# The last pass of a gMLP and cross-attention layer: only TensorE's order written by hand, rows of x three blocks deep, blocks of z two deep, and its entry, weight loads and raw tiles laid out anew

## The chip, the core and the metric

One core of a Trainium2 chip runs the whole kernel. The metric is the device time of one execution in microseconds (us), the median of several runs. The engines are named as in the profile: PE is TensorE's matmul, PEld its weight load, DVE is VectorE, ACT ScalarE, POOL GpSimd, and SP the engine whose queue issues every DMA of this kernel, in order.

## The reference, cut to what matters

One layer (DEPTH = 1) over x of 4096 rows and 1024 columns, all in float32:

```python
proj = einsum('bsd,de->bse', x, a_w_in)              # 1024 -> 768 + 768 + 256 + 1024
u, v, q_x, gate = split_cols(proj, [768, 768, 256, 1024])
tok = chunked_spatial_gating(u, v, a_w_s, a_b_s)     # gelu, norm by head, 128x128 causal mix, times u
xo = memory_cross_attention(q_x, mem_k, mem_v)       # 4 heads of 64 over a memory of 256 rows
mixed = concatenate([tok, xo]) * silu(gate)
y = einsum('bse,ed->bsd', mixed, w_out)              # 1024 -> 1024
x = layer_norm(ALPHA * x + y, ln_g, ln_b)            # over the 1024 columns of each row
```

## The kernel before

Rows are taken in 16 blocks of 256. A float32 operand is split into two parts that TensorE can multiply (`split`, L69: ACT copies the high part into the tile, then DVE subtracts it from the source and writes the low part), and a product of two split operands is three matmuls for each of four slices of the depth. The large products are done by a scheme of the Strassen kind with seven products in place of eight: sums and differences of the quarters of a block (`x_parts`, on POOL, into three `sums` tiles) are split into seven tiles of a ring (`ringp`, seven buffers named `xc`), and each of the seven is multiplied by one of seven weight tiles of 128 x 4096 elements, which lie in one large tile (`arena`). Such a product is 12 matmuls.

There are four passes over the blocks. Passes 0 and 1 (loop over `g`, L289) compute u, v, q and a part of the gate, and write them to DRAM. Beside them they prepare the weights of later passes (`prepare_slice`), split them and store them to DRAM (`wd`, `wgd`), and pass 1 computes the keys and values of the memory (`memory`, L244) with tiles of its own (`mr`, `wr`, `wt`). The third pass, here the attention pass (L393 to L538), computes the rest of the gate and the attention and writes z, the product of mixer and gate, to DRAM (`z_d`). It reads back three of the four quarters of x as split tiles (`load_x`: `xc` from `xd`), and the fourth, `a21`, raw (`x21` from `xT`), which it splits itself; after `a21` the ACT queue holds the softmax. The last pass (L541 to L727) multiplies z by `w_out`, adds x and normalizes.

Blocks of x and z come through `raw` tiles (L60, three buffers of half a block), of which a block takes two. What the planner does not decide is set by `manual_schedule`: inside it the named engines keep the order of the code. In the attention pass that is PE alone; in the last pass it was PE, DVE, ACT and POOL. Everything else, and above all SP's queue, stands in the order in which the planner put it at build time. An engine and a queue work strictly in order: what waits at the head holds all behind it.

In the last pass, block b goes through products P0 to P6, in the order of the code: `accw`, `accx`, `accq`, `accw`, `accx`, `accq`, `accw` (three accumulators; `accw` is taken up again by P3 and P6, `accx` by P4, `accq` by P5). Between them DVE reads the accumulators: t12 after P0 (`plus`, L634, from the block's rows of x, `xr`), t22 after P2, x22 after P3, x11 after P4, x12 after P5, x21 after P6; ACT copies `accx` to s1 after P1; POOL adds s1 to t12, t22 and x21. P3 can't start before t12 has read its accumulator, P5 not before t22, P6 not before x22. Beside that, the parts of block b+1 are summed on POOL and split (`nxt.sums`, `nxt.part`), and block b-1, two tiles n0 and n1 of 128 rows, is normalized: `mean` and `var` on ACT with sums along the row, a power on POOL, `norm` on ACT (one pass of 128 x 1024), `gain` and `shift` on DVE (128 x 1024 each), and then the DMA of the rows to `out`. The rows of x lie in `xr`, four tiles, that is two blocks; the tile of block b+1 is the one out of which block b-1 has just been written.

Of the kernel before, what the change touches and what calls it, by code (L numbers as in the profile page):

```python
# [35 lines left out]
def trunk_kernel(ctx, tc, xT, x, memT, w_kv, wl, wsT, bsT, ln_g, ln_b, out):  # L36
# [23 lines left out]
    def raw_tile():  # L60
        return stagep.tile([P, KH, 2 * P], F32, name="raw", tag="raw", bufs=3)
# [4 lines left out]
    def cs_tile():  # L66
        return stagep.tile([P, 512], F32, name="cs", tag="cs", bufs=6)
# [56 lines left out]
    def view(off, n):  # L124
# [8 lines left out]
        3: [13312, 17408, 21504, 25600, 0, 4096, 8192],  # L133
# [46 lines left out]
    def weights(g, load=()):  # L180
        ws = [view(o, WIDTH[g]) for o in places[g]]
        for i in load:
            nc.sync.dma_start(f(ws[i]), w_d[g][i])
        return ws
# [59 lines left out]
    def memory(pool, psum):  # L244
# [6 lines left out]
        for k in range(KD):  # L251
            mr = pool.tile([P, M], F32, name="mr")
            nc.sync.dma_start(mr, memT[:, k, :])
            wr = pool.tile([P, 2 * M], F32, name="wr")
# [3 lines left out]
            wt = pool.tile([P, 2, 2 * M], F32R, name="wt")  # L258
# [30 lines left out]
    for g in range(2):  # L289
        with tc.tile_pool(name=f"mix{g}", bufs=1, reuse_waits="tile") as pool, \  # L290
# [21 lines left out]
            for b in range(NB):  # L312
# [14 lines left out]
                if g == 1 and b == 3:  # L327
                    memory(pool, psum)
# [62 lines left out]


    with tc.tile_pool(name="att", bufs=1, reuse_waits="tile") as pool, \  # L393
# [8 lines left out]
        def x21_tile():  # L402
            return pool.tile([P, KH, P], F32, name="x21", bufs=2)

        x21s = [x21_tile()]
# [8 lines left out]
        def load_x(b):  # L414
# [4 lines left out]
            raw = x21s.pop() if x21s else x21_tile()  # L419
# [73 lines left out]
        gx = None  # L493
        with tc.manual_schedule(engines={mybir.EngineType.PE}):
            for b in range(NB):
                xs = nxt
                z1s = [load_z(b, j) for j in range(2)]
# [22 lines left out]
                gate(0, 0, 0)  # L520
                gate(0, 0, 1)
# [3 lines left out]
                gate(1, 0, 0)  # L525
                turn(p0, 0, 0)
                gate(1, 0, 1)
                turn(p1, 1, 0)
                gate(0, 1, 0)
                gate(0, 1, 1)  # L530
                turn(p2, 0, 1)
                gate(1, 1, 0)
                turn(p3, 1, 1)
                gate(1, 1, 1)
# [6 lines left out]
    with tc.tile_pool(name="fin", bufs=1, reuse_waits="tile") as pool, \  # L541
            tc.tile_pool(name="acc3", bufs=8, space=bass.MemoryType.PSUM, reuse_waits="tile") as psum:
        ws = weights(3, range(3, 7))
        H = D // 2
        xr, blocks = {}, {}

        def rows(b, i):

            for a in range(4):
                yield slice(a * 32, (a + 1) * 32), b * TB + (a % 2) * P + (2 * i + a // 2) * 32  # L550

        def load_xr(b):
            for i in range(2):
# [215 lines left out]
```

## Time and profile before

| what | value |
|---|---|
| runs | 1573.48, 1571.53, 1570.72 us; median 1571.53 |
| the profiled execution | 1573.17 us, of which the profile's span is 1571.40 |
| PE, DVE, ACT, POOL busy, share of the span | 89%, 66%, 47%, 42% |
| passes 0 and 1 | start to about 752 us |
| attention pass | about 765 to 1141 us |
| last pass | 1141 us to the end |

The row on the granted clock in the profile's second part stands at 9 (tenths of full speed) nearly throughout, with single slices at 7 where the passes meet. The digits of PE are 9 from slice 2 on and fall to 8 in the last pass. Times in the trace are microseconds from the span's start.

### The profile page before, as it was taken

How to read it: one execution, taken by the hardware profiler on the slowest of the kernel's cores; microseconds unless marked ns; L12 is line 12 of the kernel's file. 1: busy time of each engine (PE TensorE's matmuls, PEld its weight loads, DVE VectorE, ACT ScalarE, POOL GpSimd, SP SyncE). 2: the span in 40 equal slices, each digit the busy share in tenths (PEclk: the TensorE clock that was granted, in tenths of full speed). 3: DMA queues.
4: the chain of work that ended last, by engine and by line, in shares of the span. 5: the costliest groups of instructions: out<-in, count | busy, mean ns of one | idle time of the engine just before them, and what ended most of it. 6: DMA issues, size and time to landing. Idle time of an engine off the chain costs nothing.

```text
span 1571.4 us, 20805 instructions
## 1 busy us (share of the span) xinstructions
PE 1399.9 (89%) x6720; PEld 1178.0 (75%) x6720; DVE 1034.1 (66%) x2098; ACT 746.2 (47%) x1597; POOL 658.4 (42%) x515
## 2 busy tenths in 40 slices
PE   2799999999999999999499999999969888888884
PEld 2677776777778878878399999999947666666663
DVE  5788778777478867776256666666635656565555
ACT  4555555555355555555154444444515444444442
POOL 4645443444254345443044333433524454544442
PEclk9899999999999999999799999999979999999997
DMA  6468677756988585858977777777683444353523
GB/s 200 139 175 218 168 224 202 197 144 201 359 265 279 185 281 184 274 168 260 401 240 210 205 201 204 191 209 191 168 288 94 124 118 136 106 150 104 148 77 98
DMA packets 313326, 305.88 MB, mean 195 GB/s; under 512 B 147072, under 2 KB 275328, under 8 KB 310912
## 3 DMA queue, kind: packets, MB, share of 16 engines
q1 hardware_dynamic: 313216, 304.55, 66.0%
q8 instruction: 53, 0.87, 0.2%
q14 instruction: 57, 0.47, 0.1%
HBM read 183.38 MB, written 121.11 MB: 194 GB/s over the span
## 4 chain that ended last, share of the span: by engine, by line
PE 37%; DVE 18%; DMA 17%; POOL 8%; issue 7%; ACT 6%; SPq 5%; POOLq 0%; ACTq 0%; DVEq 0%
PE gate L189 16%; PE accw L189 7%; DVE xc L71 5%; PE accx L189 5%; PE accq L189 3%; DMA xr<-x 3%; DMA out<-xr 2%; DMA raw<-xT 2%; ACT vg L379 2%; DMA raw<-wl 2%; PE at L471 2%; PE sc L433 2%; ACT xc L70 2%; PE pt L451 2%; POOL cs L689 2%
## 5 line engine op out<-in xcount | busy, mean ns | idle before, releaser
L189 PE MATMUL accw<-arena,xc 128*128 128x512 f32 x1728 | 455.1, 413 | 93.5 <-ACT xc L70 34.1
L189 PEld LDWEIGHTS accw<-arena,xc 128*128 128x128 f32 x1728 | 334.3, 197 | 187.5 <-ACT xc L70 36.6
L189 PE MATMUL accx<-arena,xc 128*128 128x512 f32 x1152 | 299.8, 402 | 17.5 <-ACT arena L70 12.1
L189 PE MATMUL gate<-arena,xc 128*128 128x384 f32 x1536 | 291.4, 342 | 13.6 <-ACT xc L70 13.6
L189 PE MATMUL accq<-arena,xc 128*128 128x512 f32 x1152 | 292.2, 398 | 10.1 <-DVE cs L634 10.0
L189 PEld LDWEIGHTS gate<-arena,xc 128*128 128x128 f32 x1536 | 265.7, 190 | 14.0 <-ACT xc L70 13.8
L189 PEld LDWEIGHTS accx<-arena,xc 128*128 128x128 f32 x1152 | 218.2, 192 | 72.8 <-ACT arena L70 12.5
L189 PEld LDWEIGHTS accq<-arena,xc 128*128 128x128 f32 x1152 | 215.1, 189 | 64.4 <-DVE cs L634 14.9
L71 DVE TENSOR_TENSOR xc<-sums,xc 128x512 fp32r<-128x512 f32 x192 | 155.0, 809 | 136.1 <-ACT xc L70 135.5
L70 ACT CAST xc<-sums 128x512 fp32r<-128x512 f32 x192 | 118.2, 617 | 215.2 <-POOL sums L576 92.8
L71 DVE TENSOR_TENSOR xc<-raw,xc 128x512 fp32r<-128x512 f32 x144 | 112.1, 779 | 27.8 <-ACT xc L70 27.8
L511 POOL TENSOR_TENSOR z<-z,cs 128x384 f32<-128x384 f32 x64 | 72.5, 1133 | 131.7 <-DVE cs L509 70.6
L379 ACT ACTIVATE vg<-vg,nm,rs 128x128 f32<-128x128 f32 x192 | 77.7, 483 | 73.9 <-DVE nm L376 73.8
L70 ACT CAST xc<-raw 128x512 fp32r<-128x512 f32 x144 | 88.8, 616 | 25.9 <-PE accw L189 13.3
L445 POOL TENSOR_TENSOR sums<-sums,sm 128x512 f32<-128x512 f32 x48 | 49.3, 1041 | 98.5 <-DVE sm L444 93.9
L79 POOL TENSOR_TENSOR sums<-raw 128x512 f32<-128x512 f32 x32 | 43.2, 1350 | 109.2 <-DMA raw<-xT 62.0
L375 POOL TENSOR_TENSOR rs<-rs,mhalf 128x6 f32<-128x6 f32 x32 | 48.4, 1512 | 94.2 <-DVE rs L374 94.1
L715 POOL TENSOR_TENSOR xr<-xr,cs 128x512 f32<-128x512 f32 x16 | 26.1, 1633 | 126.5 <-DVE xr L634 125.6
L442 ACT ACTIVATE sums<-sc,nm 128x256 f32<-128x256 f32 x96 | 44.3, 472 | 67.1 <-DVE nm L438 67.1
L615 ACT ACTIVATE xr<-xr,nmean,rs 128x1024 f32<-128x1024 f32 x32 | 39.8, 1243 | 65.0 <-DVE nmean L614 53.9
L689 POOL TENSOR_TENSOR cs<-cs 128x512 f32<-128x512 f32 x16 | 26.2, 1638 | 105.3 <-DVE cs L634 105.3
L84 POOL TENSOR_TENSOR sums<-raw 128x512 f32<-128x512 f32 x32 | 45.4, 1419 | 54.1 <-DVE xc L71 51.8
(128 smaller groups left out, 2011.4 us busy)
## 6 DMA issues: line engine op xcount, KB each, us to landing
raw<-xT SPq DMA_DIRECT2D x64, 512.0 KB, 5.8
wd<-wc SPq DMA_DIRECT2D x56, 512.0 KB, 4.8
arena<-wd SPq DMA_DIRECT2D x14, 2048.0 KB, 14.2
xd<-xc SPq DMA_DIRECT2D x48, 512.0 KB, 4.8
xc<-xd SPq DMA_DIRECT2D x48, 512.0 KB, 4.5
raw<-wl SPq DMA_DIRECT2D x38, 512.0 KB, 4.1
raw<-zd SPq DMA_DIRECT2D x32, 512.0 KB, 3.9
xr<-x SPq DMA_DIRECT2D x128, 128.0 KB, 3.1
```

The source lines that it names most:

```text
L70: nc.scalar.copy(hi, src)
L71: nc.vector.tensor_tensor(lo, src, f(hi), op=ALU.subtract)
L79: tt(s1, a21, a22, op=ALU.add)
L84: tt(s3, a11, a21, op=ALU.subtract)
L189: nc.tensor.matmul(acc, t[:, a, k, :], w[:, b, k, :], start=first and k == 0 and i == 0, stop=last and k == KH - 1 and i == 2, skip_group_ ...
L375: nc.gpsimd.tensor_tensor(rs, rs, mhalf.rearrange("p (h c) -> p h c", c=2), op=ALU.pow)
L379: nc.scalar.activation(vg[:, h, c, :], vg[:, h, c, :], AF.Identity, bias=nm[:, h, c:c + 1], scale=rs[:, h, c:c + 1])
L442: nc.scalar.activation(p[:, e, :], ps[:, e, :], AF.Exp, bias=nm[:, e:e + 1], scale=SCALE, accum_out=sm[:, e:e + 1])
L445: nc.gpsimd.tensor_tensor(p, p, sm.unsqueeze(2).broadcast_to([P, 2, M]), op=ALU.mult)
L511: nc.gpsimd.tensor_tensor(z, z, g, op=ALU.mult)
L615: nc.scalar.activation(self.r, self.r, AF.Identity, bias=self.nmean, scale=self.rs)
L689: add(t22, t22, s1, op=ALU.add)
```

## The change

- **Tiles and pools.** `raw` tiles: four buffers for three; `cs` tiles five for six. `memory` takes its staging from `raw` and `wc` tiles and has none of its own. The `wc` pool is closed after pass 1, and in its place stands a pool for two `xr` tiles (`first_xr`). The fourth quarter of x in the attention pass is a `raw` tile (the left half of its columns) for the `x21` tile.
- **Weights of the last pass.** Weights 0 to 2 are loaded in blocks 4, 7 and 10 of the attention pass, ahead of its gates, and pinned there in program order (before: called after blocks 3, 6 and 9, and free for the planner). In the last attention block the gates of the second half come first, and weights 3 and 4 are loaded in the middle of that block into the places that these set free. The places of weights 3 to 5 change for that.
- **Depth.** Rows of x: block 0 and every third block use `first_xr`, the others four tiles of the last pass, so that a tile is taken again after three blocks. Pairs of z are loaded two blocks ahead (`pairs`), the first two during the last two attention blocks.
- **Order.** Only PE's order is by hand in the last pass.
- **Normalization.** `norm` is gone: `gain` is (r + nmean) * lg and `shift` is r * rs + lb, both scalar_tensor_tensor on DVE over 128 x 1024. The calls of n0 and n1 stand elsewhere in the code.

```diff
@@ pools
-    wring = ctx.enter_context(tc.tile_pool(name="wring", bufs=2))
+    front = ExitStack()
+    wring = front.enter_context(tc.tile_pool(name="wring", bufs=2))
-        return stagep.tile([P, KH, 2 * P], F32, name="raw", tag="raw", bufs=3)
+        return stagep.tile([P, KH, 2 * P], F32, name="raw", tag="raw", bufs=4)
-        return stagep.tile([P, 512], F32, name="cs", tag="cs", bufs=6)
+        return stagep.tile([P, 512], F32, name="cs", tag="cs", bufs=5)
-        3: [13312, 17408, 21504, 25600, 0, 4096, 8192],
+        3: [13312, 17408, 21504, 0, 4096, 25600, 8192],
@@ memory
-            mr = pool.tile([P, M], F32, name="mr")
+            raw = raw_tile().rearrange("p k c -> p (k c)")
+            mr, wr = raw[:, :M], raw[:, M:3 * M]
@@ between pass 1 and the attention pass
+    front.close()
+    first_xr = ctx.enter_context(tc.tile_pool(name="xr0", bufs=2, reuse_waits="tile"))
+    def load_z_pair(b):
+        zv = z_d[b].rearrange("k p t -> p k t")
+        return load_pair(zv[:, :KH, :], zv[:, KH:, :])
@@ attention pass
-            raw = x21s.pop() if x21s else x21_tile()
+            raw = raw_tile()[:, :, :P]
+                order = ((0, 0), (1, 0), (0, 1), (1, 1))
+                if b == NB - 1:
+                    order = ((0, 1), (1, 1), (0, 0), (1, 0))
                 if b + 1 < NB:
                     nxt = load_x(b + 1)
+                if b in (4, 7, 10):
+                    weights(3, (b // 3 - 1,), pinned=True)
+                if b == NB - 3:
+                    load_xr(0, first_xr, 2)
+                elif b >= NB - 2:
+                    pairs.append(load_z_pair(b - NB + 2))
...
+                if b == NB - 1:
+                    weights(3, (3, 4))
...
-                if b in (3, 6, 9):
-                    weights(3, (b // 3 - 1,))
@@ last pass
-        ws = weights(3, range(3, 7))
+        ws = weights(3, (5, 6))
-            def norm(self):
-                nc.vector.tensor_tensor(self.nmean, self.nmean, self.rs, op=ALU.mult)
-                nc.scalar.activation(self.r, self.r, AF.Identity, bias=self.nmean, scale=self.rs)
             def gain(self):
-                nc.vector.tensor_tensor(self.r, self.r, lg, op=ALU.mult)
+                nc.vector.scalar_tensor_tensor(self.r, self.r, self.nmean, lg, op0=ALU.add, op1=ALU.mult)
             def shift(self):
-                nc.vector.tensor_tensor(self.r, self.r, lb, op=ALU.add)
+                nc.vector.scalar_tensor_tensor(self.r, self.r, self.rs, lb, op0=ALU.mult, op1=ALU.add)
-        with tc.manual_schedule(engines={T_.PE, T_.DVE, T_.Activation, T_.Pool}):
+        with tc.manual_schedule(engines={mybir.EngineType.PE}):
             for b in range(NB):
-                    load_xr(b + 1)
+                    if (b + 1) % 3:
+                        load_xr(b + 1, pool, 4)
+                    else:
+                        load_xr(b + 1, first_xr, 2)
+                if b + 2 < NB:
+                    pairs.append(load_z_pair(b + 2))
```

Where this moves instructions is seen in the built programs. First SP's queue where the attention pass begins. In these rows `wgd`, `kd`, `qd` are weights, keys and queries of that pass, `xd` the split quarters of x, `x_7243` the raw fourth quarter of block 0, `wd_0` to `wd_2` the weights 0 to 2 of the last pass (2 MB each). Before:

```order
L418 DMA xc<-xd_2_156 128x1024
L490 DMA arena<-kd_203 128x1024
L426 DMA arena<-qd_106 128x4x256
L183 DMA arena<-wd_0_79 128x4096
L183 DMA arena<-wd_1_80 128x4096
L183 DMA arena<-wd_2_81 128x4096
L390 DMA z1d_104<-u 256x1x384
L239 DMA gxd_137<-gt 32x8x64 x4
L390 DMA z1d_105<-u 256x1x384
L426 DMA arena<-qd_107 128x4x256
L420 DMA x_7243<-xT 128x4x128
```

Now, at the same place, `raw` from `xT` by L442 being the fourth quarter:

```order
L440 DMA xc<-xd_2_156 128x1024
L512 DMA arena<-kd_203 128x1024
L448 DMA arena<-qd_106 128x4x256
L442 DMA raw<-xT 128x4x128
L412 DMA xr<-x 32x1024 x3
L442 DMA raw<-xT 128x4x128
L412 DMA xr<-x 32x1024 x2
L440 DMA xc<-xd_0_157 128x1024
L412 DMA xr<-x 32x1024 x3
L440 DMA xc<-xd_1_158 128x1024
```

The three weight loads are gone from here: `wd_0` now stands between the raw quarter of block 5 and the split quarters of block 2, `wd_1` between those of blocks 8 and 5, `wd_2` between those of blocks 11 and 8, about three blocks earlier than they are called. The raw quarter of block 0 stands 26 rows above the load of `qd_106`, in pass 1, those of blocks 1 and 2 behind it; the two shown here are of blocks 3 and 4. And eight loads of block 0's `xr` (128 KB each) stand here.

Second, the same queue in the middle of the last pass, with the numbers of the tiles: `xr_11785` and `xr_11790` are the two tiles of block 3 in the program before, `zd6` and `zd7` the blocks 6 and 7 of z. Before:

```order
L110 DMA raw_12306<-zd6_144 128x4x256
L556 DMA xr_11965<-x 32x1024 x4
L111 DMA raw_12307<-zd6_144 128x4x256
L623 DMA out<-xr_11785 32x1024 x4
L556 DMA xr_12135<-x 32x1024 x4
L623 DMA out<-xr_11790 32x1024 x4
L110 DMA raw_12481<-zd7_145 128x4x256
```

Here `xr_12135` is a tile of block 5. Now, with `xr_11777` and `xr_11782` the tiles of block 3 and `xr_12290`, `xr_12295` those of block 6:

```order
L113 DMA raw_12130<-zd6_144 128x4x256
L639 DMA out<-xr_11777 32x1024 x4
L412 DMA xr_12290<-x 32x1024 x4
L112 DMA raw_12300<-zd7_145 128x4x256
L639 DMA out<-xr_11782 32x1024 x4
L412 DMA xr_12295<-x 32x1024 x4
L113 DMA raw_12301<-zd7_145 128x4x256
```

Behind the output of block 3 stood the rows of block 5, now those of block 6; beside it stood the second half of z of block 6, now that of block 7 is loaded.

Third, DVE in one block of the last pass as it now stands, from t12 of block 4 (`cs_11999`) to x12 of block 4; `xc` rows are the splits of block 5's parts 0 to 4, L634 and L637 are gain and shift of n1 of block 2 (`xr_11611`), by the planner's order:

```order
L658 SCALAR_TENSOR_TENSOR cs_11999<-xr_11777,accw_11962 128x512
L615 TENSOR_SCALAR nmean_11946<-nmean_11946 128x1
L73 TENSOR_TENSOR xc_12007<-sums_11983,xc_12007 128x512
L620 TENSOR_SCALAR rs_11947<-rs_11947 128x1
L634 SCALAR_TENSOR_TENSOR xr_11611<-xr_11611,nmean_11946,lg_11429 128x1024
L73 TENSOR_TENSOR xc_12030<-raw_11787,xc_12030 128x512
L637 SCALAR_TENSOR_TENSOR xr_11611<-xr_11611,rs_11947,lb_11430 128x1024
L658 SCALAR_TENSOR_TENSOR cs_12045<-xr_11782,accq_12010 128x512
L73 TENSOR_TENSOR xc_12053<-sums_11982,xc_12053 128x512
L722 TENSOR_TENSOR xr_11782<-accw_11962,cs_12045 128x512
L73 TENSOR_TENSOR xc_12073<-sums_12056,xc_12073 128x512
L658 SCALAR_TENSOR_TENSOR xr_11777<-xr_11777,accx_11986 128x512
```

The rows that belong to one stretch of the program before, from its t12 on (`cs_12357`); L614 is the small product that ACT's `norm` waited for:

```order
L634 SCALAR_TENSOR_TENSOR cs_12357<-xr_12135,accw_12320 128x512
L600 TENSOR_SCALAR rs_12303<-rs_12303 128x1
L71 TENSOR_TENSOR xc_12363<-sums_12341,xc_12363 128x512
L71 TENSOR_TENSOR xc_12381<-raw_12306,xc_12381 128x512
L614 TENSOR_TENSOR nmean_12302<-nmean_12302,rs_12303 128x1
L595 TENSOR_SCALAR nmean_12304<-nmean_12304 128x1
L634 SCALAR_TENSOR_TENSOR cs_12400<-xr_12140,accq_12366 128x512
L71 TENSOR_TENSOR xc_12404<-sums_12340,xc_12404 128x512
L618 TENSOR_TENSOR xr_11960<-xr_11960,lg_11425 128x1024
L600 TENSOR_SCALAR rs_12305<-rs_12305 128x1
L697 TENSOR_TENSOR xr_12140<-accw_12320,cs_12400 128x512
```

Before, n0 was multiplied by the gain only after t22; now n0 is finished before t12 and n1 between t12 and t22.

## Rows read from the trace of the kernel before

**Rows 1.** Busy time by stage: length, then engines busy, PE clock, DMA share, GB/s
```profile
752.00:806.00 54.00, 31.10 (x166) 29.42 (x165) 18.28 (x46) 16.17 (x40) 10.61 (x10) 0.75 0.90 337
806.00:1141.00 335.00, 334.20 (x2153) 331.57 (x2152) 217.85 (x469) 159.94 (x454) 135.02 (x125) 1.00 0.75 201
1164.60:1551.60 387.00, 336.00 (x1308) 257.98 (x1308) 224.24 (x347) 169.13 (x267) 173.77 (x135) 0.94 0.43 120
1551.60:1571.40 19.80, 0.04 (x1) 0.00 (x0) 11.87 (x20) 2.48 (x2) 2.36 (x3) 0.62 0.32 83
```

**Rows 2.** Timeline of the start: start, duration, engine, line, operation, [idle before <-releaser]
```profile
22.12 1.26 POOL L79 TENSOR_TENSOR sums<-raw 128x512 f32<-128x512 f32 x1 [2.95 <-DMA raw<-xT]
...
48.44 0.79 PE L189 MATMUL accx<-arena,xc 128*128 128x512 f32 x1 [12.08 <-ACT arena L70]
```

**Rows 3.** Timeline where the attention pass begins, block 0
```profile
753.15 3.44 SPq L183 DMA_DIRECT2D arena<-wd  x3
...
766.61 4.87 PE L189 MATMUL gate<-arena,xc 128*128 128x384 f32 x24
...
785.39 0.62 ACT L70 CAST xc<-x 128x512 fp32r<-128x512 f32 x1 [25.89 <-DMA x<-xT]
...
786.06 4.29 PE L189 MATMUL gate<-arena,xc 128*128 128x384 f32 x12 [13.62 <-ACT xc L70]
```

**Rows 4.** Timeline of the attention pass: block 1's first gate, and one `xc` load ahead of block 14
```profile
805.95 4.33 PE L189 MATMUL gate<-arena,xc 128*128 128x384 f32 x24
...
1066.03 2.87 SPq L418 DMA_DIRECT2D xc<-xd  x2
```

**Rows 5.** Where the last pass begins: two timeline rows, one row of 3 us windows
```profile
1163.87 0.69 DVE L634 SCALAR_TENSOR_TENSOR cs<-xr,accw 128x512 f32<-128x512 f32 x1 [18.96 <-DMA xr<-x]
...
1164.61 5.49 PE L189 MATMUL accw<-arena,xc 128*128 128x512 f32 x12 [14.91 <-DVE cs L634]
...
1148.00:1151.00 3.00, 1.70 (x8) 1.03 (x6) 0.00 (x0) 0.65 (x2) 0.00 (x0) 1.00 1.00 426
```

**Rows 6.** Last pass: PE's P3, P5 and the next P3; waits after 1160 us
```profile
1411.16 3.03 PE L189 MATMUL accw<-arena,xc 128*128 128x512 f32 x12 [2.43 <-ACT junk L599]
...
1419.24 3.07 PE L189 MATMUL accq<-arena,xc 128*128 128x512 f32 x12 [1.55 <-DVE cs L634]
...
1437.44 5.46 PE L189 MATMUL accw<-arena,xc 128*128 128x512 f32 x12 [3.23 <-DVE rs L600]
...
DVE cs L634 <- DMA xr<-x: 32.6, 15, 19.0
```

**Rows 7.** Groups from 1160 us on: line, operation, count, busy us, mean ns
```profile
L615 ACT ACTIVATE xr<-xr,nmean,rs 128x1024 f32<-128x1024 f32 x32 | 39.8, 1243 | 65.0 <-DVE nmean L614 53.9 <-DMA out<-xr 11.1
L621 DVE TENSOR_TENSOR xr<-xr,lb 128x1024 f32<-128x1024 f32 x32 | 39.4, 1231 | 0.1
...
L71 DVE TENSOR_TENSOR xc<-raw,xc 128x512 fp32r<-128x512 f32 x45 | 31.0, 690 | 22.3 <-ACT xc L70 22.3
...
L576 POOL TENSOR_TENSOR sums<-raw 128x512 f32<-128x512 f32 x15 | 19.3, 1289 | 0.0
```

**Rows 8.** Timeline: DVE and POOL at the same moment, both with two operands in SBUF
```profile
1394.25 2.31 DVE L618 TENSOR_TENSOR xr<-xr,lg 128x1024 f32<-128x1024 f32 x1
...
1395.44 2.25 POOL L690 TENSOR_TENSOR cs<-cs 128x512 f32<-128x512 f32 x1
```

**Rows 9.** Timeline of the end: last matmuls, DVE's last statistics and last instruction
```profile
1548.68 2.96 PE L189 MATMUL accw<-arena,xc 128*128 128x512 f32 x12
...
1560.64 1.28 DVE L607 BATCH_NORM_STATS2 st<-xr 128x6 f32<-128x512 f32 x2
...
1565.80 1.23 DVE L621 TENSOR_TENSOR xr<-xr,lb 128x1024 f32<-128x1024 f32 x1
```

**Rows 10.** DMA groups of the page: issues, KB each, median us to landing
```profile
xc<-xd SPq DMA_DIRECT2D x48, 512.0 KB, 4.5
...
raw<-zd SPq DMA_DIRECT2D x32, 512.0 KB, 3.9
```

More of the change, by code (lines that the diff above doesn't have):

```diff
@@ L493, in trunk_kernel @@
         gx = None
+        pairs = []
         with tc.manual_schedule(engines={mybir.EngineType.PE}):
@@ L542, in trunk_kernel @@
             tc.tile_pool(name="acc3", bufs=8, space=bass.MemoryType.PSUM, reuse_waits="tile") as psum:
-        ws = weights(3, range(3, 7))
+        ws = weights(3, (5, 6))
         H = D // 2
[L545 to L553, printed above, removed]
-                t = xr[b, i] = pool.tile([P, D], F32, name="xr", bufs=4)
-                for s, r0 in rows(b, i):
-                    nc.sync.dma_start(t[s, :], x[r0:r0 + 32, :])
+        blocks = {}
         class Parts:
             def __init__(self, b):
-                self.r0, self.r1 = load_pair(z_d[b].rearrange("k p t -> p k t")[:, :KH, :],
-                                             z_d[b].rearrange("k p t -> p k t")[:, KH:, :])
+                self.r0, self.r1 = pairs[b]
                 self.tiles = []
@@ L675, in trunk_kernel @@
                 n0.var()
+                n1.mean()
                 nxt.part(0)
@@ L681, in trunk_kernel @@
                 nc.scalar.copy(s1, ax)
+                n0.gain()
+                n1.var()
                 nxt.part(1)
-                n0.norm()
-                n1.mean()
                 product(aw, xs[3], ws[3], False)
@@ L689, in trunk_kernel @@
                 add(t22, t22, s1, op=ALU.add)
-                add(t12, t12, s1, op=ALU.add)
+                n0.shift()
                 nxt.part(2)
-                n0.gain()
-                n1.var()
                 nxt.sums(3)
@@ L697, in trunk_kernel @@
                 nc.vector.tensor_tensor(x22, aw, t22, op=ALU.add)
+                add(t12, t12, s1, op=ALU.add)
+                n1.gain()
                 nxt.part(3)
-                n0.shift()
-                n1.norm()
                 product(aq, xs[5], ws[5], False)
@@ L705, in trunk_kernel @@
                 nxt.part(4)
-                n1.gain()
+                n1.shift()
                 product(aw, xs[6], ws[6], False)
@@ L710, in trunk_kernel @@
                 nxt.part(5)
-                n1.shift()
-                def last(aw=aw, x21=x21, s1=s1):
-                    plus(x21, aw, x21)
-                    add(x21, x21, s1, op=ALU.add)
-                n0, n1 = Norm(b, 0), Norm(b, 1)
+                n0, n1, last = Norm(b, 0), Norm(b, 1), Last(aw, x21, s1)
                 cur = nxt
             n0.stats()
-            n0.norm()
-            last()
             n0.gain()
             n0.shift()
+            last.c21()
             n1.stats()
-            n1.norm()
             n1.gain()
```

80 lines of the change are left out of this document (46 added, 34 removed).

## The prediction

> **What bounds the kernel now.** I read four views: busy time by stage, then the timeline where a stage begins or ends, then the waits of the last pass, then its groups by operation.
>
> By stage, TensorE (PE) does nothing but work in 335 us of the attention pass: 334.20 busy, 15 blocks at 22.3 us each [rows 1]. That stretch can't get shorter by other waits going away, and the change takes no matmul out. Four places are left where PE isn't full. The start: PE stands 12.08 us at 48.44, where ACT's split of weights comes last [rows 2]. The attention entry: 31.10 busy of 54 us, at a mean clock of 0.75 [rows 1]. The last pass: 336.0 of 387 us, clock 0.94 [rows 1], with 14.91 us of idling right at its entry [rows 5]. And the tail, 19.8 us without PE [rows 1].
>
> In the last pass these 387 us hold 1308 matmuls [rows 1], 109 products of twelve: 3.55 us each, 24.9 us a block of seven. Products start 2.80 us apart at best (2.96 with the end of the pipeline [rows 9]), so 19.6 us. Each of the waits in a block is short (2.43 before P3, 1.55 before P5 [rows 6]), and behind one of 3.23 us the product itself took 5.46 in place of 2.96 [rows 6], as at the lower of the two clock levels, 1.2 in place of 2.4 GHz (0.94 is the mean of the stage). So a block pays a wait and, where it was long, up to 2.5 us on top. DVE (224 us), POOL (174) and ACT (169) are far from full in it [rows 1]: order and latency bound this pass, not an engine's sum. DVE's t12, which P3 waits for, stood 32.6 us in all on the rows of x [rows 6].
>
> **The change part by part.** The profiled execution is 1573.17 us, span 1571.40; the terms are made against it, and the median of the runs lies 1.6 lower.
>
> *Start.* A fourth raw tile lets a load go ahead that POOL waited for: at least the 2.95 us in [rows 2]; at most what of PE's 12.08 is left beside that, 9. I take the middle: -6 (-3 to -9).
>
> *Attention entry.* Before, three 2 MB weights were issued at 753.15 ahead of the raw quarter of block 0; ACT's cast stood 25.89 us for it at 785.39, with the softmax behind it, and PE stood 13.62 at 786.06 [rows 3]. Block 0's gate begins at 766.61 [rows 3], block 1's at 805.95 [rows 4]: 39.3 us for a block that needs 22.3, a loss of 17.0. Now the quarter is loaded in pass 1 and no weight stands before it. Next late is the turn of the first softmax, by some 2 us, and the clock, for 0.5: -14.5. The bound above is -17.0; for the other, half the wait might move to the block-0 z and gate loads that share the queue with rows of x: -10.
>
> *Weights in the attention pass.* They now stand between a raw quarter and the split quarters of an earlier block. A 2 MB load with the DMA to itself takes 4.9 us by 426 GB/s [rows 5]; the split quarters behind it were issued at 1066.03 [rows 4] for a gate near 1096 (805.95 + 13 x 22.32), 30 us ahead, and land in 4.5 [rows 10]. Cover gone, one weight costs its 4.9. So 0 (0 to +5).
>
> *Last pass, entry and blocks.* From 1141.0 to 1551.64 (the end of the last product [rows 9]) it is 410.6 us now. The floor is 112 products x 2.80 + 0.2 = 313.8. How close? The entry first: block 0's rows of x stood behind the scatter of z and the weights (t12 at 1163.87 after 18.96 of waiting, PE 14.91 idle, then 12 matmuls in 5.49 [rows 5]); now they and two blocks of z are loaded in the attention pass, weights 3 and 4 ahead of it, 5 and 6 needed 14 and 16.8 us into it, at 4.9 each. Nothing is left to wait for. The last pass's DMA share is 0.43 [rows 1].
>
> Now a steady block, time 0 at the start of P0. Durations: split 0.69, shift 1.23, POOL's sum 1.29 [rows 7], the read of an accumulator 0.69 [rows 5]; gain counts as shift. Before t12 DVE has x21, gain and shift of n0 and one split, and can lose one POOL sum: 0.69 + 2 x 1.23 + 0.69 + 1.29 + t12's 0.69 = 5.8, with small instructions 5.9; P3 needs it at 8.4. To t22 come two splits, gain and shift of n1 and t22: 4.5, one or two waits for a POOL sum, 2.1: 12.5; P5 needs it at 14.0. To x22 one split, POOL's t22+s1 and x22 itself, 2.5: 15.0; P6 needs it at 16.8. So PE doesn't wait in the order that now stands; ACT loses 39.8 us of norm [rows 7], and gain and shift stay one pass each at about 1.23.
>
> What can bind is the loop of DVE and POOL. Where both worked from SBUF with two operands, gain took 2.31 against shift's 1.23, and POOL's sum 2.25 against 1.29 [rows 8, 7]: one stood while the other worked. Per block, seven splits, four gains and shifts and eight sums, laid end to end: 7 x 0.69 + 4 x 1.23 + 8 x 1.29 = 20.07, above PE's 19.6; not all of it meets. So 20.0 us a block, 0.4 over the floor in 14 blocks: 313.8 + 5.6 = 319.4, a gain of 91.2. Ends: the floor, 96.8; the other end, 80, is 0.8 us more in each of 14 blocks.
>
> [...]
>
> *Tail.* Behind the last matmul: x21 0.69, a shift in front of it 1.23, POOL's sum 1.29, statistics of one half 0.64 [rows 9] and small steps near 1, gain and shift 2.46: 7.3, say 7.5; the write behind DVE's last instruction took 1571.4 - 1565.80 - 1.23 = 4.4 [rows 9]. 11.9 against 19.8 [rows 1]: -8 (-6 to -9).
>
> *Passes 0 and 1 otherwise.* Memory's staging goes through tiles that the weights' preparation uses; a burst may hold loads of x or free them. No row prices it. Nearest is a wait like that of the start, half of 12.08 either way: 0 (-6 to +6).
>
> Sum: -6 - 14.5 + 0 - 91.2 - 8 + 0 = -119.7. 1573.17 - 119.7 = 1453.5; 1.6 lower as a median, 1452. All ends together would give 1434 and 1484.
>
> **The rivals.**
> *B, DVE and POOL bind.* For: [rows 8], a sum of 20.07 above PE's 19.6, and a free order that doesn't place POOL's sums beside DVE's reads of accumulators (one SBUF operand, no loss). Against: those reads (5 of 0.69 a block) leave room. 1.1 us a block beyond the forecast, a start lost on eight sums by some 0.14 each: 21.1, x 14 = +15: 1467.
> *C, PE alone.* Little meets, 19.6 a block (-5.6), the start gives 9 and the burst 6: 1438. For: the slacks of 1.5 to 2.5 us above.
> *D, the queues' order.* DVE, ACT and POOL now run in the planner's order; POOL's three sums for the block after next may stand ahead of x21+s1. A wait of 2.5 us a block stays, about what P3 has now [rows 6], without low clock: 2.1 x 14 = +29 over the forecast, 1481; with one low-clock product in six, 1487.
> *F, the entry's wait only moves.* Block 0's z and gates stand behind the eight loads of rows of x in the queue; the 14.5 us come back: 1466.
> *E, slower than before.* Each half of z now has its own place in the queue behind an output; POOL's sums of the block after next need it at 15.6 in the block. Issued at 4.3, landing in 3.9 [rows 10], it is there at 8.2, 7.4 early. If outputs that wait for shift, at the head of the queue, put it off, POOL holds x21+s1, the mean, t22 and P5, in each block. It eats the gain of 119.5 at 8.5 us in each of 14 blocks, that is 28.5 us a block, or a half of z that is there 16 us later than worked out; at 30 us a block it is 1592. Against it: the DMA share of 0.43 [rows 1], and that two pairs are loaded ahead.
>
> **How the numbers follow.** Forecast 0.49 (1442 to 1461), B 0.23, C 0.11, F 0.08, D 0.06, E 0.03. The time is the forecast's, 1452. The range must hold 0.8: forecast, B with its spread, F and the half of C above 1438; 1438 to 1476 leaves out D, E, half of C and what B may reach above, near 0.2. A measurement of this kernel can tell about 0.2% from no change, 3 us. All cases but E lie far below the time before; E's 0.03 is 0.02 slower and 0.01 about equal: faster 0.97, same 0.01, slower 0.02.
>
> **What the profile will show.** Right: by stage, the attention pass still at 22.3 us a block, block 1's gate some 22 to 27 us behind block 0's, no wait of ACT for the raw quarter; the last pass's blocks 20 us apart, PE's clock near 1.00 there, waits before P3, P5 and P6 under 0.5 us; ACT without the norm group; gain and shift at 1.23 where alone; a tail of 12 us. B would show blocks of 21 us with gains and POOL's sums over 2 us in mean. D shows a wait of PE for a DVE instruction that itself waited for POOL; F a wait of 10 us or more in the first attention block under another DMA's name; E waits of POOL for loads of z in every block. I am wrong if PE's matmuls in the last pass are slower than 2.96 a product without any wait, or if the attention blocks grow by the weights.

## The result and the profile after

The changed kernel takes 1453.96 us (median; 1452.82 to 1454.39) against 1571.53: a ratio of 0.9248, 95% interval 0.9227 to 0.9269. The profiled execution took 1454.39 us, its span is 1452.70. 1452 was forecast, in a range of 1438 to 1476.

Busy time by stage of the changed kernel (length, then PE, PEld, DVE, ACT, POOL, PE clock, DMA share, GB/s), to be held against [rows 1]:

```profile
740.00:792.00 52.00, 31.29 (x169) 29.35 (x168) 19.93 (x51) 16.51 (x42) 10.62 (x10) 0.77 0.81 271
792.00:1127.00 335.00, 334.07 (x2152) 331.45 (x2151) 215.96 (x467) 159.06 (x454) 135.62 (x125) 1.00 0.78 222
1127.00:1441.00 314.00, 313.82 (x1344) 252.30 (x1344) 261.81 (x335) 141.35 (x244) 202.56 (x138) 1.00 0.54 166
1441.00:1452.70 11.70, 0.04 (x1) 0.00 (x0) 5.99 (x9) 0.00 (x0) 2.79 (x2) 0.65 0.36 90
```

The third row is the result in one line: all 1344 matmuls of the last pass in 314.00 us, 313.82 busy, clock 1.00. PE all but never waits there. The attention pass is as long as it was, 335 us. DVE is busy in the last pass 262 us of 314 now and POOL 203, both denser than before; a part of that is time in which one stands for the other (below).

By milestones of PE:

| stretch | before | after | difference | forecast |
|---|---|---|---|---|
| start to first gate | 766.61 | 757.52 | -9.1 | -6 (start) + 0 (passes) |
| first gate to block 1's gate | 39.3 | 34.3 | -5.0 | -14.5 |
| 15 attention blocks | 335.1 | 335.4 | +0.3 | 0 |
| last pass, first to last matmul | 410.6 | 313.9 | -96.7 | -91.2 |
| tail | 19.8 | 11.65 | -8.1 | -8 |
| sum | 1571.4 | 1452.7 | -118.7 | -119.7 |

The sum came out within 1 us, and that is luck in part: the entry fell short by 9.5 us, the last pass gave 5.5 more than forecast and the stretch ahead of the first gate 3.1 more.

One block of the last pass after the change, timeline (start, duration, engine, line, operation, and in brackets the idle time before it and its releaser):

```profile
1308.85 0.68 DVE L658 SCALAR_TENSOR_TENSOR cs<-xr,accw 128x512 f32<-128x512 f32 x1
...
1312.08 2.96 PE L196 MATMUL accw<-arena,xc 128*128 128x512 f32 x12
...
1312.77 2.31 DVE L637 SCALAR_TENSOR_TENSOR xr<-xr,rs,lb 128x1024 f32<-128x1024 f32 x1
...
1315.00 0.67 DVE L658 SCALAR_TENSOR_TENSOR cs<-xr,accq 128x512 f32<-128x512 f32 x1
...
1317.45 0.69 DVE L722 TENSOR_TENSOR xr<-accw,cs 128x512 f32<-128x512 f32 x1 [1.18 <-POOL cs L716]
1317.68 2.96 PE L196 MATMUL accq<-arena,xc 128*128 128x512 f32 x12
```

P0 begins at 1303.68 (the second half of a row of 24 matmuls from 1300.88). t12 is done 5.9 us later (P3 begins at 8.4), t22 at 12.0 (P5 at 14.0), x22 at 14.5 (P6 at 16.8). The walk of the prediction had 5.9, 12.5 and 15.0.

Where the attention pass begins, timeline of the changed kernel, against [rows 3]:

```profile
744.82 6.30 SPq L412 DMA_DIRECT2D xr<-x  x3
...
757.52 4.80 PE L196 MATMUL gate<-arena,xc 128*128 128x384 f32 x24
...
760.80 3.16 SPq L246 DMA_DIRECT2D gxd<-gt  x4
...
768.32 2.48 DVE L459 TENSOR_REDUCE nm<-sc 128x2 f32<-128x512 f32 x4 [14.18 <-DMA gxd<-gt]
...
774.70 1.11 PE L473 MATMUL pt<-ident,sums 128*128 128x128 f32 x4 [9.33 <-POOL sums L467]
```

The wait for the raw quarter is gone, and another has taken most of its place. DVE's first maximum of the softmax stands 14.18 us for the last store of pass 1 (`gxd<-gt`), as the profile has it; why it needs that store isn't shown. The store is issued at 760.80, behind the eight loads of rows of x, of which the first three alone held SP's queue 6.30 us. PE waits 9.33 us for the softmax.

### The profile page after: what moved, and what is told of

Its sections match the earlier page's. It is cut to its first block, busy times and chain, and to the rows that moved or that the text cites. A ratio compares the mean times of both kernels' runs of the same rounds, so it can differ in the third digit from the quotient of the medians.

```text
span 1452.7 us, 20674 instructions
## 1 busy us (share of the span) xinstructions
PE 1364.6 (94%) x6720; PEld 1167.9 (80%) x6720; DVE 1066.3 (73%) x2066; ACT 713.2 (49%) x1565; POOL 692.6 (48%) x515
## 4 chain that ended last, share of the span: by engine, by line
PE 72%; DVE 9%; DMA 9%; issue 3%; ACT 3%; POOL 3%; SPq 0%; DVEq 0%; POOLq 0%; ACTq 0%
PE accw L196 20%; PE gate L196 18%; PE accx L196 14%; PE accq L196 12%; DMA raw<-xT 3%; DVE xc L73 2%; PE at L493 2%; PE sc L455 2%; PE pt L473 2%; DMA wd<-wc 2%; ACT vg L386 1%; DMA xr<-x 1%; DVE arena L73 1%; PE mixed L393 1%; DVE wc L73 1%
## 5 line engine op out<-in xcount | busy, mean ns | idle before, releaser
L196 PE MATMUL accw<-arena,xc 128*128 128x512 f32 x1728 | 432.7, 399 | 25.1 <-ACT xc L72 23.2
L196 PEld LDWEIGHTS accw<-arena,xc 128*128 128x128 f32 x1728 | 324.8, 190 | 103.5 <-ACT xc L72 23.2
L73 DVE TENSOR_TENSOR xc<-sums,xc 128x512 fp32r<-128x512 f32 x192 | 167.5, 873 | 74.2 <-ACT xc L72 74.1
L72 ACT CAST xc<-raw 128x512 fp32r<-128x512 f32 x160 | 99.2, 620 | 103.9 <-PE accx L196 42.1
L73 DVE TENSOR_TENSOR xc<-raw,xc 128x512 fp32r<-128x512 f32 x160 | 139.0, 869 | 14.6 <-ACT xc L72 14.5
L219 POOL TENSOR_TENSOR cs<-cs 128x512 f32<-128x512 f32 x32 | 43.2, 1350 | 71.1 <-ACT cs L218 71.0
L81 POOL TENSOR_TENSOR sums<-raw 128x512 f32<-128x512 f32 x32 | 44.4, 1386 | 67.2 <-DMA raw<-xT 27.3
L393 PEld LDWEIGHTS mixed<-vn,wm 128*128 128x128 f32 x288 | 47.9, 196 | 30.1 <-ACT vn L72 16.8
L393 PE MATMUL mixed<-vn,wm 128*128 128x256 f32 x288 | 52.8, 294 | 18.8 <-ACT vn L72 16.4
L89 POOL TENSOR_TENSOR sums<-raw,sums 128x512 f32<-128x512 f32 x32 | 52.8, 1651 | 34.4 <-DVE xc L73 26.6
```

The costliest lines, as they stand in the source:

```text
L72: nc.scalar.copy(hi, src)
L73: nc.vector.tensor_tensor(lo, src, f(hi), op=ALU.subtract)
L81: tt(s1, a21, a22, op=ALU.add)
L89: tt(s4, a12, s2, op=ALU.subtract)
L196: nc.tensor.matmul(acc, t[:, a, k, :], w[:, b, k, :], start=first and k == 0 and i == 0, stop=last and k == KH - 1 and i == 2, skip_group_ ...
L219: nc.gpsimd.tensor_tensor(s5, s5, s1, op=ALU.add)
```

## Experiments

Times are medians; ratios are against the kernel before on the same chip. "Last pass" is from its first to its last matmul in the profiled execution. A profile is one execution: in order4, norm_act, norm_order4, pool4 and the changed kernel, whose code ahead of the last pass is the same, that pass begins between 1124.4 and 1127.2 us, so a difference of 2 or 3 us between two profiles says little.

| run | us | ratio (95%) | last pass | tail |
|---|---|---|---|---|
| changed kernel | 1453.96 | 0.9248 (0.9227 to 0.9269) | 313.9 | 11.7 |
| xr_pinned | 1444.05 | 0.9173 (0.9158 to 0.9188) | 313.9 | 11.7 |
| best3 | 1439.95 | 0.9156 (0.9139 to 0.9173) | 314.4 | 11.6 |
| raw3 | 1493.19 | 0.9479 (0.9455 to 0.9503) | 317.5 | 12.1 |
| mem_stage | 1457.30 | 0.9254 (0.9240 to 0.9269) | 318.0 | 11.7 |
| order4 | 1456.77 | 0.9246 (0.9227 to 0.9264) | 315.8 | 13.2 |
| depth1 | 1452.24 | 0.9238 (0.9224 to 0.9252) | 313.9 | 11.7 |
| depth1_order4 | 1455.18 | 0.9252 (0.9234 to 0.9269) | 316.3 | 14.4 |
| norm_act | 1463.01 | 0.9306 (0.9286 to 0.9325) | 321.1 | 14.2 |
| norm_order4 | 1497.09 | 0.9522 (0.9503 to 0.9540) | 350.0 | 20.2 |
| depth1_norm_order4 | 1495.92 | 0.9511 (0.9496 to 0.9526) | 348.7 | 20.4 |
| before_free | 1494.06 | 0.9497 (0.9480 to 0.9513) | 338.7 | 14.3 |
| pool4 | 1499.40 | 0.9539 (0.9521 to 0.9558) | 359.1 | 13.5 |

### The attention entry: is it the queue?

**xr_pinned**, block 0's rows of x kept in the place of the code:

```diff
-                    load_xr(0, first_xr, 2)
+                    load_xr(0, first_xr, 2, pinned=True)   # tc.keep_in_program_order on each load
```

> The changed kernel with one difference: the eight loads of block 0's rows of x, which the planner had put into the queue where the attention pass begins, keep the place of the code, in block 13 of that pass. In the changed kernel DVE's first maximum of the softmax waits 14.18 us for the DMA gxd<-gt, whose issue stands at 760.80 behind those loads (the first three of them held the queue 6.30 us from 744.82), and PE then waits 9.33 us at 774.70. Theory 1, the queue: the stores come forward by the time of the loads, the maximum no longer waits, and the time falls by 7 to 11 us to 1443 to 1447; the first gate to the second block's gate takes 23 to 27 us in place of 34.3. Rival: what holds the stores is the split quarters and keys ahead of them or the data itself; then the time stays within 3 us of 1454, and the wait has another name.

10 us less (12 by the ratios), as the queue would have it. Its timeline:

```profile
739.60 6.59 SPq L444 DMA_DIRECT2D raw<-xT  x2
...
749.40 3.95 SPq L246 DMA_DIRECT2D gxd<-gt  x4
...
758.39 2.48 DVE L461 TENSOR_REDUCE nm<-sc 128x2 f32<-128x512 f32 x4 [8.28 <-DMA gxd<-gt]
...
764.78 1.12 PE L475 MATMUL pt<-ident,sums 128*128 128x128 f32 x4 [3.77 <-POOL sums L469]
```

The store is issued 11.4 us earlier, and PE's wait falls from 9.33 to 3.77. The time is as Theory 1 had it, the place only in part: from the first gate (752.86) to block 1's gate (781.50) it is 28.6 us, not 23 to 27, that is 5.7 us less than 34.3, and the other 4.7 us of the two profiles lie ahead of the first gate. What is left of the wait has the same form: two raw quarters of later blocks hold the queue 6.59 us.

**best3**, besides that the quarters of attention blocks 1 to 15 in the place of the code:

```diff
-                nc.sync.dma_start(f(t), d)
+                i_ = nc.sync.dma_start(f(t), d)
+                if b:
+                    tc.keep_in_program_order(i_)      # the same for the raw quarter
```

> The changed kernel with block 0's rows of x in block 13, as in xr_pinned, and besides with the split quarters and the raw quarter of x of attention blocks 1 to 15 kept where the code has them, one block ahead, so that the stores of pass 1 follow the first block's weights at once. In xr_pinned DVE's first maximum still waits 8.28 us for gxd<-gt, whose issue at 749.40 stands behind two raw quarters that hold the queue 6.59 us and three split quarters; PE then waits 3.77 us. Theory: that wait goes, 4 to 6 us with the lower clock: 1438 to 1441. Rival: the raw quarters and split quarters are now late for blocks 1 and 2, or the wait goes to the queries: within 2 us of 1444, or slower.

In its timeline DVE's wait is 2.56 us, and PE waits no more for the softmax:

```profile
740.47 6.63 SPq L246 DMA_DIRECT2D gxd<-gt  x4
...
752.31 1.29 DVE L465 TENSOR_REDUCE nm<-sc 128x2 f32<-128x512 f32 x2 [2.56 <-DMA gxd<-gt]
...
760.44 0.60 PE L479 MATMUL pt<-ident,sums 128*128 128x128 f32 x4
```

First gate (752.26) to block 1's gate (775.54) is 23.3 us, within 1 us of a steady block (22.3) and where the prediction had expected the change to be. best3 is the fastest kernel of this study, 0.9156 against the changed kernel's 0.9248, with intervals apart. Between best3 and xr_pinned the intervals overlap; the profiles' 5.4 us from gate to gate (28.6 to 23.3) are seen in one execution each.

### Raw tiles and the memory's staging

**raw3**, three raw tiles for four:

```diff
-        return stagep.tile([P, KH, 2 * P], F32, name="raw", tag="raw", bufs=4)
+        return stagep.tile([P, KH, 2 * P], F32, name="raw", tag="raw", bufs=3)
```

> The changed kernel with three raw tiles in place of four. At 400 us the changed kernel has 1593 matmuls behind it, the kernel before 1515, that is some 17 us more. Theory 1: the fourth raw tile gives that lead in the start and in pass 0; without it 10 to 20 us are lost there, and in the last pass the two blocks of z ahead no longer fit, which brings waits for z back: 1465 to 1500. Rival: the lead comes from elsewhere (the planner's new order), the last pass needs only three: within 4 us of 1454.

By the ratios some 36 us more, in the range of Theory 1, though more than its 10 to 20 are lost early. Its waits of PE (us in total, times, longest), up to 100 us and from 480 to 800 us:

```profile
PE accx L196 <- ACT arena L72: 14.0, 1, 14.0
...
PE mixed L393 <- ACT vn L72: 20.5, 2, 13.4
```

In the changed kernel these are 8.54 and 3.26 us at the start and 8.4 from 480 to 800 us.

Its busy times from 60 to 400 us, with the number of instructions:

```profile
60.00:400.00 340.00, 324.88 (x1422) 257.85 (x1421) 261.71 (x580) 185.66 (x409) 150.06 (x107) 0.99 0.70 188
```

The same row of the changed kernel (PE 1483 matmuls for 1422; the counts in the expectation took matmuls at window borders twice, the lead is alike):

```profile
60.00:400.00 340.00, 333.04 (x1483) 268.68 (x1482) 274.32 (x591) 191.59 (x420) 157.55 (x112) 0.99 0.77 215
```

The loss lies ahead of the attention pass, whose first gate begins at 788.13 in place of 757.52; in the last pass only 3.6 us are added, although POOL waits 15.0 us for z there. So the passes 0 and 1 need the fourth tile, as the expectation had it in its first half; the z blocks, its second half, don't. raw3 comes later to its last pass than even the kernel before, which has three tiles too (1141.04): there the fourth quarter of x and the memory's staging had their own, which is the likely reason; it was not tried for raw3.

**mem_stage**, the memory's two raw operands in tiles of their own:

```diff
-            raw = raw_tile().rearrange("p k c -> p (k c)")
-            mr, wr = raw[:, :M], raw[:, M:3 * M]
+            mr = pool.tile([P, M], F32, name="mr")
+            wr = pool.tile([P, 2 * M], F32, name="wr")
```

> The changed kernel with the memory's two staging tiles given back as tiles of their own (the split one stays in the tile shared with the weights). In the changed kernel PE stands 8.0 us at 449.77 and 2.6 at 455.97 and then takes 5.24 us for 12 matmuls. Theory 1: the staging through the raw tiles, at the place where pass 1 begins, takes loads of x from their buffers; given back, 6 to 12 us come back: 1442 to 1448, and 250 matmuls or more stand in the 60 us from 420 (239 in the changed kernel). Rival: the hiccup is pass 1's own beginning (the chain of v's norm into the mix), or the shared weight tile; then within 3 us of 1454.

Same as the changed kernel. The wait between the passes didn't go; the changed kernel's row, then mem_stage's:

```profile
449.77 0.79 PE L393 MATMUL mixed<-vn,wm 128*128 128x256 f32 x2 [7.97 <-ACT vn L72]
```

```profile
450.88 0.79 PE L393 MATMUL mixed<-vn,wm 128*128 128x256 f32 x2 [9.93 <-ACT vn L72]
```

The staging is not its cause. The second stop, of 2.6 us, is gone, and 246 matmuls in place of 233 stand in the 60 us from 420 (each counted once), short of the sign's 250; nothing of it is left in the time, with a last pass 4 us longer. What causes the long wait stays open: ACT's splits of weights, one of which waits 2.68 us for a store of its tile at 445.01 in the changed kernel, stand ahead of v's cast, but that was not tried.

### The last pass: order, depth or norm?

Each of the three was taken back alone, then in pairs, then all together.

**order4**, all four engines in the order of the (changed) code:

```diff
-        with tc.manual_schedule(engines={mybir.EngineType.PE}):
+        with tc.manual_schedule(engines={T_.PE, T_.DVE, T_.Activation, T_.Pool}):
```

> The changed kernel with DVE, ACT and POOL held to the order of the code in the last pass, too; buffers and loads stay as changed. Theory 1, depth: what PE waited for in the last pass were rows of x and blocks of z, so that with the deeper buffers it stays within 5 us of 1454. Theory 2, order: the four queues by hand were the cause of the waits before P3 and P5; then 1.5 to 4 us come back in each block, some of them with the lower clock: 1475 to 1520.

**depth1**, rows of x taken again after two blocks, z one block ahead:

```diff
-                    if (b + 1) % 3:
-                        load_xr(b + 1, pool, 4)
+                    if (b + 1) % 2:
+                        load_xr(b + 1, pool, 2)
...
-                if b + 2 < NB:
-                    pairs.append(load_z_pair(b + 2))
+                    pairs.append(load_z_pair(b + 1))
```

> The changed kernel with the old depth in the last pass: rows of x in four tiles that are taken again after two blocks, blocks of z loaded one block ahead; the order stays free, norm stays away. With the order by hand and this depth kept as changed the time had hardly moved, so depth is the suspect. Theory 1, depth: the waits of the kernel before come back, 1 to 3.5 us a block before P3 (DVE's t12 on the DMA of rows of x) and P5, some with the lower clock: 1475 to 1530. Theory 2, either is enough, a free order or deep buffers: within 5 us of 1454. Theory 3, norm: ACT's lost pass is what counts; within 5 us of 1454 here, too.

**depth1_order4**, both edits.

> The changed kernel with the old depth of rows of x and blocks of z and all four engines in the order of the code; norm stays away. If depth is needed only where the order is fixed (DVE's t12 then waits for rows of x), 10 to 40 us more than 1454: 1464 to 1495; if norm is the part that makes a fixed order costly, within 5 us of 1454.

All three take what the changed kernel takes, within the intervals; the two profiles with a fixed order show 3 to 5 us more in last pass and tail, which the medians don't. Neither the depth nor the free order is needed alone, nor the one where the other is missing.

**norm_act**, the normalization as before:

```diff
-                nc.vector.scalar_tensor_tensor(self.r, self.r, self.nmean, lg, op0=ALU.add, op1=ALU.mult)
+                nc.vector.tensor_tensor(self.nmean, self.nmean, self.rs, op=ALU.mult)
+                nc.scalar.activation(self.r, self.r, AF.Identity, bias=self.nmean, scale=self.rs)
+                nc.vector.tensor_tensor(self.r, self.r, lg, op=ALU.mult)
```

> The changed kernel with the normalization as before (ACT's pass over 128 x 1024, then gain and shift as products and sums of two operands); order free, buffers deep. Theory 1, depth (or order): the 40 us of ACT lie beside PE's work, the blocks stay at 19.6 us, and only the tail grows, by two passes of 1.24 and their hand-overs, 2 to 4 us: 1455 to 1460. Theory 3, norm: the longer chain from mean to output keeps the tile of x, and 0.5 to 2 us a block come back: 1463 to 1490.

9 us more, at the lower edge of Theory 3: 7.2 in the blocks, that is 0.45 in each, and 2.5 in the tail.

**norm_order4**, norm_act and order4 together:

> The changed kernel with norm on ACT and all four engines in the order of the code; rows of x and blocks of z stay deep. Order alone cost nothing, norm alone 9 us, the two with the old depth 43 us. If norm and order together make the loss, 1488 to 1497; if the deep buffers are what absorbs a fixed order, 1460 to 1470.

43 us more. **depth1_norm_order4**, all three:

> The changed kernel with all three taken back in the last pass: old depth, norm on ACT, and all four engines in the order of the code (which is that of the changed code); entry, weights and raw tiles stay as changed. It shows whether the three together carry the last pass's gain: if so a block takes 22 to 25 us again, 1490 to 1545. If it stays within 10 us of 1454, the gain came from the entry, from the weights' loads or from the new places in the code, and the three are not needed.

Again 42 us: depth adds nothing. So it is the pair: norm on ACT *and* a fixed order, 36 us in the last pass and 8.5 in the tail. How, is seen in the timeline of norm_order4:

```profile
1309.48 1.24 ACT L635 ACTIVATE xr<-xr,nmean,rs 128x1024 f32<-128x1024 f32 x1 [0.40 <-DVE nmean L634]
1310.63 1.14 ACT L619 ACTIVATE junk<-xr,nmean 128x1024 bf16<-128x1024 f32 x1
1310.76 1.23 DVE L636 TENSOR_TENSOR xr<-xr,lg 128x1024 f32<-128x1024 f32 x1 [1.37 <-ACT xr L635]
...
1311.77 0.60 ACT L72 CAST xc<-raw 128x512 fp32r<-128x512 f32 x1
...
1312.40 0.69 DVE L73 TENSOR_TENSOR xc<-raw,xc 128x512 fp32r<-128x512 f32 x1 [0.35 <-ACT xc L72]
1313.01 0.68 DVE L660 SCALAR_TENSOR_TENSOR cs<-xr,accq 128x512 f32<-128x512 f32 x1
...
1313.75 3.06 PE L196 MATMUL accq<-arena,xc 128*128 128x512 f32 x12 [1.55 <-DVE cs L660]
```

DVE's gain waits 1.37 us for norm (1.24), which itself waits for DVE's small product of `nmean` and `rs`. Norm and the squares (1.14) of the block before also stand on ACT ahead of a cast of the next block's part, and DVE's split waits 0.35 for that cast. t22, whose accumulator has been ready since 1306.2 (P2 ended there), stands behind gain and split. Over the whole pass and the tail the list of waits has for DVE:

```profile
DVE xr L636 <- ACT xr L635: 44.4, 32, 1.6
DVE xc L73 <- ACT xc L72: 32.1, 29, 1.9
```

The second wait is there without norm, too (29.6 us in depth1_order4, which loses nothing); what norm adds in a fixed order is the first, and with a free order 9.6 of it are left (norm_act). P5 waits for t22, 1.55 us in this block, the same wait as in [rows 6]. For PE in the last pass the list gives:

```profile
PE accq L196 <- DVE cs L660: 19.3, 13, 1.8
PE accw L196 <- DVE xr L725: 4.4, 12, 0.4
```

23.7 of the 36 us. Some 11 more are busy time: the same 1344 matmuls take 325.0 us in this pass for 313.8 in the changed kernel. With either half of the pair gone the wait goes too: the last pass takes 321.1 us with a free order (norm_act) and 315.8 without norm (order4).

**before_free**, the kernel before with the one edit of the order:

```diff
-        with tc.manual_schedule(engines={T_.PE, T_.DVE, T_.Activation, T_.Pool}):
+        with tc.manual_schedule(engines={T_.PE}):
```

> The kernel before with one difference: in the last pass only PE's order is by hand. Entry, weights, depth, norm and the places of the code stay. If a free order gives most of the last pass's gain, its blocks close in 20 to 21 us in place of 24.9, the entry of 15 us stays: 1490 to 1515. If the order matters only with the other parts, 1555 to 1575; if the rows of x a block late are the cause, 1540 to 1570 with DVE waiting for them.

As the first case had it: 79 us of the 118 come from this one line, as long as norm is there; order4 showed that without norm it is worth nothing. In its steady stretch PE is busy 276.91 of 280 us (the row is that of 280 us from 1180):

```profile
1180.00:1460.00 280.00, 276.91 (x1176) 219.76 (x1175) 243.97 (x319) 157.29 (x249) 176.54 (x123) 1.00 0.53 153
```

The entry stays as it was, timeline:

```profile
1165.07 5.16 PE L189 MATMUL accw<-arena,xc 128*128 128x512 f32 x12 [16.41 <-DVE cs L634]
```

And DVE's t12 waits for rows of x there, but no longer in each block as in [rows 6] (list of waits, us in total, times, longest):

```profile
DVE cs L634 <- DMA xr<-x: 15.8, 2, 14.2
```

So those waits for rows of x in the kernel before were not for want of tiles: the tiles are as many here. They fit late outputs: a tile's load, which stands behind an output, is issued at 1432.33 for a t12 at 1436.61 in the kernel before, 4.3 us ahead, and at 1311.32 for one at 1323.15 in before_free, 11.8 us ahead. What norm_order4's last pass (350.0) still is below that of the kernel before (410.6) has two parts by subtraction: the entry, 14.9 of waiting and 2.5 of slow matmuls [rows 5], and some 43 us. For those the likeliest cause is where the calls of n0 and n1 stand in the code, since a fixed order follows it; depth is excluded (depth1_norm_order4), but the fourth raw tile and the weights' loads differ too, and none of the three was tried by itself. What the trace of the kernel before shows is a longer wait of DVE's splits for ACT's casts in the last pass, 100.0 us in place of the 32.1 above:

```profile
DVE xc L71 <- ACT xc L70: 100.0, 57, 3.0
```

### What binds next

**pool4**, four more sums on POOL in each block:

```diff
                 add(t12, t12, s1, op=ALU.add)
+                for _ in range(2):
+                    add(t12, t12, s1, op=ALU.subtract)
+                    add(t12, t12, s1, op=ALU.add)
```

> The changed kernel with four additional sums on POOL in each block of the last pass (s1 is taken from t12 and added again, twice), which changes the result only by rounding. It tests what binds next. By the account of the prediction, in which sums of POOL and passes of DVE that read two operands from SBUF stand end to end (20.07 us a block), 4 x 1.29 more give 25.2 us a block: 1535 to 1545. If they meet only in part and POOL's own time is the limit (12.7 us of 19.6 busy now, 17.8 then), blocks stay near 20: 1454 to 1465.

Neither. A block takes 22.4 us (359.1/16): of 5.16 us added, as four sums alone, 2.8 show. Its row of busy times for the 290 us from 1130, in which POOL works 260 and PE 262:

```profile
1130.00:1420.00 290.00, 261.54 (x1094) 204.57 (x1093) 228.46 (x263) 113.06 (x199) 260.10 (x165) 0.99 0.54 155
```

Groups of the changed kernel from 1160 to 1420 us (count, busy us, mean ns):

```profile
L637 DVE SCALAR_TENSOR_TENSOR xr<-xr,rs,lb 128x1024 f32<-128x1024 f32 x26 | 46.7, 1797 | 2.2 <-POOL rs L621 2.2
L634 DVE SCALAR_TENSOR_TENSOR xr<-xr,nmean,lg 128x1024 f32<-128x1024 f32 x26 | 40.6, 1560 | 0.0
L73 DVE TENSOR_TENSOR xc<-raw,xc 128x512 fp32r<-128x512 f32 x40 | 39.3, 983 | 0.0
...
L591 POOL TENSOR_TENSOR sums<-raw 128x512 f32<-128x512 f32 x13 | 21.1, 1625 | 1.0
...
L658 DVE SCALAR_TENSOR_TENSOR xr<-xr,accx 128x512 f32<-128x512 f32 x14 | 9.5, 675 | 0.0
```

In the changed kernel shift takes 1.80 in the mean and gain 1.56, where either takes 1.28 alone (the last shift of the tail, at 1447.07), the split 0.98 for 0.69, and this sum on POOL 1.63 for 1.29 [rows 7]. The two engines do stand in each other's way, and PE doesn't notice: if their loop is what sets the block in pool4, it had some 2.3 us a block to spare (5.16 - 2.8). That holds for sums at this place. They stand ahead of t12's last user, x12, and DVE waits for them there in nearly every block (pool4, list of waits):

```profile
DVE xr L737 <- POOL cs L726: 34.1, 14, 2.6
```

End to end 25.2 us were due in pool4 (25.0 with the seven sums and two powers of a block that the code has), and 22.4 came. A part of POOL's sums runs beside DVE's reads of accumulators, which keep their 0.675 us (last row of the groups). Two rows from the timeline of the changed kernel show it, a read that lies wholly within a sum, both at what they take alone:

```profile
1303.49 1.30 POOL L596 TENSOR_TENSOR sums<-raw 128x512 f32<-128x512 f32 x1 [0.62 <-DVE xc L73]
...
1303.88 0.69 DVE L658 SCALAR_TENSOR_TENSOR xr<-xr,accw 128x512 f32<-128x512 f32 x1 [0.20 <-PE accw L196]
```

The Trainium skill, "SBUF — State Buffer", section "Who interferes with whom", has it so: a DVE instruction with at most one input in SBUF, outside the modes that use both ports, doesn't contend with GpSimd. The trace agrees, with these 1.30 and 0.69 us.

## Why the prediction was right, point by point

- **Start and passes 0 and 1, -6 and 0:** -9.1 together. PE's stop at the weights' split, one of 12.08 us before [rows 2], is two now, and the eleven matmuls behind it come 2.6 us earlier, not 6. In the timeline, first the changed kernel, then the kernel before:

```profile
42.62 0.80 PE L196 MATMUL accx<-arena,xc 128*128 128x512 f32 x1 [8.54 <-ACT arena L72]
...
47.19 4.99 PE L196 MATMUL accx<-arena,xc 128*128 128x512 f32 x11 [3.26 <-DVE arena L73]
```

```profile
49.79 4.89 PE L189 MATMUL accx<-arena,xc 128*128 128x512 f32 x11
```

  The larger part is the step that had no row: loads go ahead all through pass 0 (PE busy 333.04 of 340 us from 60 us, 324.88 with three tiles), and a part of it is lost again between the passes, where PE stands 8.0 and 2.6 us. That the two terms together came near is luck.
- **Attention entry, -14.5:** -5.0; this step failed. "Next late is the turn of the first softmax, by some 2 us" was 9.33 us. The walk followed the raw quarter and the loads that the block needs, not the stores of pass 1 behind the eight loads of rows of x in the same queue, and DVE's maximum waits for such a store. Rival F had the place (those loads) and not the victim: it named block 0's z and gates. xr_pinned and best3 gave the time back, and best3 with it the 23 us that the prediction had expected.
- **Weights in the attention pass, 0:** +0.3 in 15 blocks.
- **Last pass, -91.2:** -96.7. The entry went as worked out: PE waits 0.45 us at its first product and nowhere after. The term of 0.4 us a block, for DVE and POOL standing end to end, was mis-sized: it is 0. Its sum had an error, too: the code has seven sums a block on POOL, not eight (four for the parts, three with s1), so that end to end it is 18.78 us, and 19.88 with the two powers at 0.55; and the new gain and shift take 1.28 alone, not 1.23. Rival C (19.6 a block) is what happened there. B's sign, gains and POOL's sums over 2 us in the mean, is not there: gains have 1.56 and POOL's sums at most 1.70. They are above what they take alone, but that costs PE nothing; pool4 shows how much room is left.
- **Tail, -8:** -8.1.
- What the prediction did not do was to say which part of the change carries the last pass. It counted the rows of x (t12's 32.6 us) among the causes; depth1 shows that their depth is worth nothing, neither with a free nor with a fixed order.

## What to carry to other kernels

Where an engine's queue is in order, read what stands ahead of the instruction that is late, not only what it waits for: t22 and the softmax's maximum were each held by something that had nothing to do with them. Before buffers are deepened for a wait on a load, take the order or the long pass that delays the buffer's release away alone; here one line, applied to the kernel before, did two thirds of the work, and the deeper rows of x and blocks of z did nothing. In the changed kernel the free order or the removal of the long pass is enough, and either is worth little alone. The one buffer that counts is the fourth raw tile, 36 us, in the earlier passes. And a load that is hoisted ahead of its need has a price in the queue: pin it where it's needed if stores stand behind it.

## What was not expected of the hardware

A power over 128 x 1 on POOL takes 0.55 us where it begins 0.02 us ahead of a gain of DVE, and 1.52 where it begins 0.17 us behind one; the gain takes 1.28 both times. Timeline of the changed kernel's last block and tail:

```profile
1428.93 1.28 DVE L634 SCALAR_TENSOR_TENSOR xr<-xr,nmean,lg 128x1024 f32<-128x1024 f32 x1
1429.10 1.52 POOL L621 TENSOR_TENSOR rs<-rs,mhalf 128x1 f32<-128x1 f32 x1 [3.53 <-DVE rs L620]
...
1440.21 0.55 POOL L630 TENSOR_TENSOR rs<-rs,mhalf 128x1 f32<-128x1 f32 x1 [5.22 <-DVE nmean L631]
1440.23 1.28 DVE L634 SCALAR_TENSOR_TENSOR xr<-xr,nmean,lg 128x1024 f32<-128x1024 f32 x1
```

The slow one ends at 1430.62, just behind the gain's end at 1430.21: a tiny instruction on POOL waits out the long one on DVE that began before it, and the shift that needs its result waits with it. The gain here is that of the power's own tile, which DVE starts right behind `rs`. An order in which other work of DVE, one that reads an accumulator, stands between `rs` and the gain might avoid that; it wasn't tried.
